# Decoder trunk on one core: sums of weights in place, more load buffers, two units without accumulating transfers, operands at one residue

## The chip, the cores and the metric

The kernel runs on one core of a Trainium2 chip. The metric is the device time of one execution in microseconds (us). The core has a matrix engine (TensorE, "PE" in the profile, its weight loads "PEld"), VectorE (DVE), ScalarE (ACT), GpSimd (POOL) and SyncE (SP), which here only issues transfers. Each engine works through its own instructions in order.

## The reference

A trunk of two layers over 512 positions of width 1024, in float32. Layer A: a recurrent mixer (norm, projection, causal convolution of width 4, gated linear recurrence, output projection) and a SwiGLU block. Then keys and values shared by what follows; layer B: dilated sliding-window attention in three groups of heads and a second SwiGLU block. The change lies in the two SwiGLU blocks and in where tiles lie in the on-chip memory.

```python
def swiglu(h, w_in, w_out):
    g, u = jnp.split(h @ w_in, 2, axis=-1)
    return (jax.nn.silu(g) * u) @ w_out
# h: 512 x 1024, w_in: 1024 x 5632, w_out: 2816 x 1024
h = h + swiglu(rms_norm(h, norm), w_in, w_out)
```

## The kernel before

**Precision.** Every matrix is split into a high and a low half (`...h`, `...l`, type fp32r), and a product is three matmuls (`mm3`, L195 to L197): high by high, high by low, low by high. For weights, ScalarE casts the high half (L114, L145, L157) and the low half is the weight minus it: on VectorE (L116, L158), on POOL, or, in the SwiGLU input weights, by a negated copy on ScalarE (L135) to which a transfer from memory adds the weight itself (L136, issued by POOL, "accumulating transfer").

**SwiGLU input products.** The 2816 hidden columns are 22 units of 128. A unit takes two blocks of weights, `g` (tile `wr`) and `u` (tile `ur`), seen as a 2 x 2 matrix A11, A12, A21, A22 in pairs of 128 rows. Seven products instead of eight give it (Winograd's scheme): A11, A12, A22 and four sums of weights S1 to S4 on the left, B11, B21, B22 and sums T1 to T4 of activations on the right; each is 4 x 3 matmuls of 256 columns. Activations lie in `xh`/`xl` (B11, T1, B21, B22) and `th`/`tl` (T2 to T4), formed by `sums` at the end of the stage before. A unit is done in three parts: `head` (A11, S1), then the `tail` (A22, S4 and the gate) of the unit before, then `middle` (S2, A12, S3). Partial results are copied out of PSUM on ScalarE (`t`, L535). The gate needs the norm's factor in a row per position, `rb`, from `norm_factors` and `norm_rows`: small VectorE work, `dg`, and a matmul by `ones`. It is formed after the `middle` of unit 0.

**SwiGLU output products.** The hidden columns come in chunks of 4, 5, 5, 4, 4 units. The out blocks of a chunk (8 blocks, 12 or 15 matmuls of 512 columns each, left operand `wh`/`wl`, right `gh`/`gl`) are spread between the units of the next chunk, mostly two after each unit; the last chunk's come at the end.

**Weights' stream.** `Stream` holds the list of pieces in the order of use. At `get(i)` it issues the load of piece i+2 (SP's queue) and the split of piece i+1. Raw weights lie in `wr` (two buffers, for units' `g`, out blocks and all other projections alike) and `ur` (one buffer); split weights in `wh`/`wl` (three each), `a2h`/`a2l` (two) and `sh`/`sl` (three). The sums are formed in two tiles `s`, (S1, S2) and (S3, S4). A framework lays out the order of every engine's instructions and the semaphores before the run, from its own estimates; a tile's buffer is free when all who read it are done.

**Where tiles lie.** Pools are stacked: `keep` (h, `xh`, `xl`, `par`, `ident`, `ones`, `ssum`), then the weights, then the stage's pool; on the other side of the memory, "right", the pools of `hgh` and of `gh`, closed by a `pad` tile of 8 floats. `Pool` rounds a tile to 64 bytes a partition.

Other stages that the profile shows: the projections of the recurrent layer (`xh` by `wh`, 512 columns), its output (`hgh`), keys, values and queries (L820 to L822: weights on the right, `xh`, or its copy by phase `xp`, on the left), attention.

Of the kernel before, what the change touches and what calls it, by code (L numbers as in the profile page):

```python
# [20 lines left out]
F32 = mybir.dt.float32  # L21
F32R = mybir.dt.float32r
# [3 lines left out]
ALU = mybir.AluOpType  # L26
# [3 lines left out]
T = 512  # L30
KB = 8
HID = 2816
HB = HID // 128
# [48 lines left out]
class Stream:  # L82
# [6 lines left out]
        self.nl = self.ns = self.halved = 0  # L89

    def _load(self, i):
        ap, kind = self.pieces[i]
        if kind == "unit":
            return self._load_unit(i)
        r = self.pool.tile([128, 1024], F32, name=f"wr{i}", tag="wr", bufs=2)
# [23 lines left out]

    def _load_unit(self, i):  # L120
        g = self.pool.tile([128, 1024], F32, name=f"wr{i}", tag="wr", bufs=2)
        u = self.unit_pool.tile([128, 1024], F32, name=f"ur{i}", tag="ur", bufs=1)
        self.raw[i] = (g, u)
        return [lambda t=t, a=a: self.nc.sync.dma_start(t, a) for t, a in zip((g, u), self.pieces[i][0])]

    def _split_unit(self, i):

        nc, pool, up = self.nc, self.pool, self.unit_pool
        g, u = self.raw.pop(i)

        def halves(t):
            return t.rearrange("q (k e c) -> q e k c", e=2, c=128)

        def negated_plus(lo, raw, ap):
            nc.scalar.mul(lo, raw, -1.0)  # L135
            nc.gpsimd.dma_start(lo, ap, accum_op=ALU.add)  # L136

        with self.tc.high_priority():
            a1h = pool.tile([128, 1024], F32R, name=f"wh{i}", tag="wh")
            a1l = pool.tile([128, 1024], F32R, name=f"wl{i}", tag="wl")  # L140
            a2h, a2l = (up.tile([128, 4, 128], F32R, name=n, tag=n, bufs=2) for n in ("a2h", "a2l"))
            (a11, a12), (a21, a22) = ([halves(t)[:, e] for e in range(2)] for t in (g, u))
            negated_plus(a1l, g, self.pieces[i][0][0])
            negated_plus(a2l, a22, halves(self.pieces[i][0][1])[:, 1])
            nc.scalar.copy(a1h, g)  # L145
            nc.scalar.copy(a2h, a22)
            s = [up.tile([128, 2, 4, 128], F32, name="s", tag="s", bufs=2) for _ in range(2)]
            sh, sl = ([up.tile([128, 2, 4, 128], F32R, name=n, tag=n, bufs=3) for _ in range(2)] for n in ("sh", "sl"))
            V = nc.vector
            for n in range(2):  # L150
                if n == 0:
                    V.tensor_tensor(s[0][:, 0], a21, a22, ALU.add)
# [4 lines left out]
                nc.scalar.copy(sh[n], s[n])  # L157
                V.tensor_tensor(sl[n], s[n], sh[n].bitcast(F32), ALU.subtract)  # L158
        a1h, a1l = halves(a1h), halves(a1l)
        self.parts[i] = {"A11": (a1h[:, 0], a1l[:, 0]), "A12": (a1h[:, 1], a1l[:, 1]), "A22": (a2h, a2l)}  # L160
        for n in range(4):
            self.parts[i][f"S{n + 1}"] = tuple(x[n // 2][:, n % 2] for x in (sh, sl))

    def start(self, n):

# [23 lines left out]
def trunk(tc, A, out):  # L189
# [8 lines left out]

    pieces = []

    def add_pieces(aps, kind=""):
        start = len(pieces)
        pieces.extend((a, kind) for a in aps)
        return start

    lru_order = [8, 9, 10, 11, 12, 0, 13, 1, 14, 2, 15, 3, 4, 5, 6, 7]
# [4 lines left out]
    def ffn_pieces(wi, wo):  # L211

        def out_step(c, m):
            c0 = 128 * sum(CHUNKS[:c])
            return "out", c, m, add_pieces([A[wo][m][:, c0:c0 + 128 * CHUNKS[c]]])
# [12 lines left out]
        return steps  # L228
# [7 lines left out]
    with tc.tile_pool(name="keep", bufs=1) as kp, tc.tile_pool(name="wts", bufs=3) as wp, \  # L236
# [94 lines left out]


        close_hg, hg = right_pool(tc, "hg")
        with tc.tile_pool(name="lru", bufs=2, reuse_waits="tile") as lp:
            lp = Pool(lp)
            for k in range(KB):
                split(h[k], gain(C_AN, k), xh[k], xl[k])
                run(split_a if k == 0 else split_b if k == 3 else ())
# [16 lines left out]
            r = norm_factors(lp)  # L355
            rb = norm_rows(lp, r, "q", 2)


            lam = par[:, C_LAM:C_LAM + 8]
            sp8, nsp8 = (lp.tile([128, 8], F32, name=n, bufs=1) for n in ("sp8", "nsp8"))  # L360
            l1 = lp.tile([128, 8], F32, name="l1", bufs=1)
            l2 = lp.tile([128, 8], F32, name="l2", bufs=1)
            l3 = lp.tile([128, 8], F32, name="l3", bufs=1)
# [133 lines left out]
        def sums(pool, m, c):  # L497

            if m % 2 == 0:
                return  # L500
            x = [pool.tile([128, T], F32, name="x", tag=t) for t in ("gt", "ut")]
            for i in range(2):
                S.activation(x[i], h[m - 1 + i], AF.Copy, scale=gain(c, m - 1 + i))
# [20 lines left out]
        def swiglu(fp, gp, steps, after):  # L524
# [21 lines left out]
            def middle(w, pa, pc, t1):  # L546

                pb = bank("S")
                product(pa, w["S2"], "T2", False, False)
                t2 = copied(pa, "t2")  # L550
                product(pb, w["A12"], "B21", True, True)
                g = fp.tile([128, T], F32, name="gt")
                u = fp.tile([128, T], F32, name="ut")
                V.tensor_tensor(g[:, a], pb[:, a], t1, ALU.add)
                product(pa, w["S3"], "T3", False, False)
                t3 = copied(pa, "t3")
                V.tensor_tensor(u[:, b], pc[:, a], t3, ALU.add)
                return w, pa, pc, t2, g, u
# [27 lines left out]
            for kind, *step in steps:  # L586
                if kind == "unit":
                    j, p = step
                    w = ws.get(p)
                    st = head(w)  # L590
                    if pending:
                        tail(*pending.pop())
                    pending.append(middle(w, *st))
                    if j == 0:
                        r = norm_factors(fp)
                        rbs.append(norm_rows(fp, r, "o"))
                    continue
                c, m, p = step
                n, last = CHUNKS[c], c == len(CHUNKS) - 1
# [529 lines left out]
```

## Time and profile before

| | |
|---|---|
| median of three runs | 1316.86 us (1315.63 to 1318.35) |
| profiled execution | 1319.34 us, span 1317.4 us |
| instructions | 19514 |
| PE / DVE / ACT / POOL busy | 92% / 72% / 53% / 20% |
| mean granted clock of TensorE | 0.965 |
| transferred | 147.89 MB, mean 112 GB/s |

A row of a group reads: line, engine, operation, tile written <- tiles read, shapes, count, then total busy time in us and mean ns of one, then the engine's idle time before them and what ended it. A row of the timeline reads: start in us, duration in us, engine, line, operation, tiles, and in brackets the idle time before it and who ended it; "SPq" is the issue of a transfer by SP. A row of stretches reads: stretch, its length, busy us and count of PE, PEld, DVE, ACT, POOL, then TensorE's clock, the share of the transfer engines, GB/s. A matmul's duration is longer than the distance to the next one, as matmuls overlap.

The first SwiGLU block runs from about 200 to 565 us, the second from about 943 to the end.

### The profile page before, as it was taken

How to read it: one execution, taken by the hardware profiler on the slowest of the kernel's cores; microseconds unless marked ns; L12 is line 12 of the kernel's file. 1: busy time of each engine (PE TensorE's matmuls, PEld its weight loads, DVE VectorE, ACT ScalarE, POOL GpSimd, SP SyncE). 2: the span in 40 equal slices, each digit the busy share in tenths (PEclk: the TensorE clock that was granted, in tenths of full speed). 3: DMA queues.
4: the chain of work that ended last, by engine and by line, in shares of the span. 5: the costliest groups of instructions: out<-in, count | busy, mean ns of one | idle time of the engine just before them, and what ended most of it. 6: DMA issues, size and time to landing. Idle time of an engine off the chain costs nothing.

```text
span 1317.4 us, 19514 instructions
## 1 busy us (share of the span) xinstructions
PE 1218.1 (92%) x7218; PEld 1066.1 (81%) x7218; DVE 954.6 (72%) x1870; ACT 701.7 (53%) x1322; POOL 269.1 (20%) x233
## 2 busy tenths in 40 slices
PE   6779897999999999998998899899889999999998
PEld 5557686988999988876777677789788889889987
DVE  7888887766777666688755666776886776677666
ACT  5466676554454555357444555655864555555531
POOL 1444001111111111020233355531211111111100
PEclk8888899999999999998998999799999999999999
DMA  5221257566766665242332212101665667666643
GB/s 177 80 64 49 80 118 165 125 145 140 159 152 152 143 143 121 74 133 68 111 97 65 76 53 65 33 17 49 128 145 120 155 149 166 143 137 145 142 101 105
DMA packets 69694, 147.89 MB, mean 112 GB/s; under 512 B 6240, under 2 KB 30944, under 8 KB 69600
## 3 DMA queue, kind: packets, MB, share of 16 engines
q1 hardware_dynamic: 39024, 110.17, 27.3%
q0 software_dynamic: 29568, 34.61, 17.9%
q10 hardware_dynamic: 1008, 1.88, 0.5%
q8 instruction: 56, 0.92, 0.3%
q14 instruction: 38, 0.31, 0.1%
HBM read 143.49 MB, written 2.10 MB: 111 GB/s over the span
## 4 chain that ended last, share of the span: by engine, by line
issue 44%; PE 25%; DVE 16%; POOL 6%; ACT 5%; DMA 3%; POOLq 0%; SPq 0%; ACTq 0%; DVEq 0%
PE ps L196 5%; PE ps L197 5%; PE ps L195 5%; POOL a2l L136 4%; DVE kn L779 3%; PE ps L820 3%; PE ps L821 3%; PE ps L822 3%; POOL wl L136 2%; DMA wl<-in_f_in 1%; DVE xc L409 1%; ACT junk L762 1%; DVE gated L458 1%; DVE wl L116 1%; ACT wh L114 1%
## 5 line engine op out<-in xcount | busy, mean ns | idle before, releaser
L114 ACT CAST wh<-wr 128x1024 fp32r<-128x1024 f32 (+2 forms) x150 | 124.4, 831 | 191.7 <-PE ps L196 82.2
L197 PE MATMUL ps<-xh,wl 128*128 128x256 f32 (+1 forms) x544 | 179.8, 330 | 14.7 <-DMA wl<-in_f_in 14.7
L195 PE MATMUL ps<-xh,wh 128*128 128x256 f32 (+1 forms) x544 | 180.2, 332 | 8.1 <-ACT xh L279 5.9
L196 PE MATMUL ps<-xl,wh 128*128 128x256 f32 (+1 forms) x544 | 178.2, 328 | 1.5 <-DVE xl L284 1.3
L116 POOL TENSOR_TENSOR wl<-wr,wh 128x1024 fp32r<-128x1024 f32 x46 | 114.2, 2484 | 241.5 <-ACT wh L114 215.3
L136 POOL DMA_DIRECT2D a2l<-in_f_in x44 | 53.0, 1205 | 434.7 <-ACT a2l L135 386.9
L196 PE MATMUL ps<-gl,wh 128*128 128x512 f32 x352 | 139.2, 396 | 0.0
L195 PE MATMUL ps<-gh,wh 128*128 128x512 f32 x352 | 138.9, 395 | 0.0
L197 PE MATMUL ps<-gh,wl 128*128 128x512 f32 x352 | 138.9, 394 | 0.0
L197 PEld LDWEIGHTS ps<-xh,wl 128*128 128x128 f32 x544 | 105.6, 194 | 26.1 <-DMA wl<-in_f_in 17.4
L195 PEld LDWEIGHTS ps<-xh,wh 128*128 128x128 f32 x544 | 105.6, 195 | 19.2 <-ACT xh L279 5.9
L196 PEld LDWEIGHTS ps<-xl,wh 128*128 128x128 f32 x544 | 105.7, 194 | 12.4 <-DVE xl L284 2.1
L158 DVE TENSOR_TENSOR sl<-s,sh 128x1024 fp32r<-128x1024 f32 x88 | 106.9, 1217 | 1.8 <-ACT sh L157 1.7
L195 PE MATMUL ps<-th,sh 128*128 128x256 f32 x352 | 103.0, 293 | 3.3 <-ACT t L535 3.1
L157 ACT CAST sh<-s 128x1024 fp32r<-128x1024 f32 x88 | 91.8, 1045 | 18.8 <-PE ps L196 12.6
L195 PE MATMUL ps<-xh,sh 128*128 128x256 f32 x352 | 99.6, 283 | 1.1 <-ACT sh L157 1.1
L197 PE MATMUL ps<-th,sl 128*128 128x256 f32 x352 | 99.9, 284 | 0.0
L196 PE MATMUL ps<-tl,sh 128*128 128x256 f32 x352 | 99.7, 283 | 0.0
L196 PE MATMUL ps<-xl,sh 128*128 128x256 f32 x352 | 99.0, 281 | 0.0
L197 PE MATMUL ps<-xh,sl 128*128 128x256 f32 x352 | 98.8, 281 | 0.0
L116 DVE TENSOR_TENSOR wl<-wr,wh 128x512 fp32r<-128x512 f32 (+2 forms) x104 | 86.0, 830 | 14.7 <-ACT wh L114 14.5
L581 DVE TENSOR_TENSOR o<-ps,rb 128x512 f32<-128x512 f32 x80 | 55.1, 689 | 54.5 <-PE ps L197 53.1
(259 smaller groups left out, 3317.3 us busy)
## 6 DMA issues: line engine op xcount, KB each, us to landing
ur<-in_f_in SPq DMA_DIRECT2D x44, 512.0 KB, 3.8
wr<-in_f_in SPq DMA_DIRECT2D x44, 512.0 KB, 4.1
wl<-in_f_in POOLq DMA_DIRECT2D x44, 512.0 KB, 6.7
wr<-in_f_out SPq DMA_DIRECT2D x48, 256.0 KB, 2.7
wr<-in_w_q SPq DMA_DIRECT2D x24, 512.0 KB, 3.6
a2l<-in_f_in POOLq DMA_DIRECT2D x44, 256.0 KB, 5.2
wr<-in_f_out SPq DMA_DIRECT2D x32, 320.0 KB, 3.4
wr<-in_w_in SPq DMA_DIRECT2D x14, 512.0 KB, 3.6
```

Source lines behind the costliest of these rows:

```text
L114: nc.scalar.copy(hi[:, c], r[:, c])
L116: eng.tensor_tensor(lo[:, c], r[:, c], hi[:, c].bitcast(F32), ALU.subtract)
L136: nc.gpsimd.dma_start(lo, ap, accum_op=ALU.add)
L157: nc.scalar.copy(sh[n], s[n])
L158: V.tensor_tensor(sl[n], s[n], sh[n].bitcast(F32), ALU.subtract)
L195: PE.matmul(ps, wh, xh, start=first, stop=False, **k)
L196: PE.matmul(ps, wh, xl, start=False, stop=False, **k)
L197: PE.matmul(ps, wl, xh, start=False, stop=last, **k)
L581: V.tensor_tensor(o, ps, rbs[0], ALU.mult)
L779: V.scalar_tensor_tensor(dst[:, c], dst[:, c], r[:, nh * t + i:nh * t + i + 1], grow[:, g_row, :], ALU.mult, ALU.mult)
L820: PE.matmul(ps[t], xh[k][:, r], wh[:, c], start=k == 0, stop=False)
L821: PE.matmul(ps[t], xh[k][:, r], wl[:, c], start=False, stop=False)
```

## The change

1. The sums S1 to S4 are formed in place in the raw tiles: a22 = a21 + a22 (S1), a21 = a11 - a21 (S3), then, once `u` has been split, a11 = a22 - a11 (S2), a12 = a12 - a11 (S4). The tiles `s` go. One pair of `sh`/`sl` holds S3 and S1, the other S2 and S4.
2. `ur` gets two buffers; out blocks get raw tiles of their own (`or`, two), so `wr` serves units and other projections alone. For room, `ut` gets one buffer, and both tiles `x` of `sums` use the two of `gt`.
3. For units 0 and 1 of each block (`early`) the low halves of A11, A12 and A22 are subtracted on VectorE, without negated copy and accumulating transfer.
4. `norm_factors` (at unit 0) and `norm_rows` (moved to unit 1, between its `head` and the `tail` of unit 0) get high priority.
5. Sizes: `par` 128 floats instead of 104, the pad on the right 88 instead of 8, `xp` 640 instead of 516; small tiles of the recurrent stage move to a pool `few` of their own. Nothing else in these stages changes.

```diff
-        tc.nc.gpsimd.memset(pool.tile([128, 8], F32, name="pad"), 0.0)
+        tc.nc.gpsimd.memset(pool.tile([128, 88], F32, name="pad"), 0.0)
...
+        if kind == "out":
+            r = self.unit_pool.tile([128, 640], F32, name=f"or{i}", tag="or", bufs=2)
+        else:
+            r = self.pool.tile([128, 1024], F32, name=f"wr{i}", tag="wr", bufs=2)
...
-        u = self.unit_pool.tile([128, 1024], F32, name=f"ur{i}", tag="ur", bufs=1)
+        u = self.unit_pool.tile([128, 1024], F32, name=f"ur{i}", tag="ur", bufs=2)
...
-        def negated_plus(lo, raw, ap):
-            nc.scalar.mul(lo, raw, -1.0)
-            nc.gpsimd.dma_start(lo, ap, accum_op=ALU.add)
+        def split(hi, lo, raw, ap):
+            nc.scalar.copy(hi, raw)
+            if ap is None or early:
+                V.tensor_tensor(lo, raw, hi.bitcast(F32), ALU.subtract)
+            else:
+                nc.scalar.mul(lo, raw, -1.0)
+                nc.gpsimd.dma_start(lo, ap, accum_op=ALU.add)
...
-            negated_plus(a1l, g, self.pieces[i][0][0])
-            negated_plus(a2l, a22, halves(self.pieces[i][0][1])[:, 1])
-            nc.scalar.copy(a1h, g)
-            nc.scalar.copy(a2h, a22)
-            s = [up.tile([128, 2, 4, 128], F32, name="s", tag="s", bufs=2) for _ in range(2)]
...
-                if n == 0:
-                    V.tensor_tensor(s[0][:, 0], a21, a22, ALU.add)
-                    V.tensor_tensor(s[0][:, 1], s[0][:, 0], a11, ALU.subtract)
-                else:
-                    V.tensor_tensor(s[1][:, 0], a11, a21, ALU.subtract)
-                    V.tensor_tensor(s[1][:, 1], a12, s[0][:, 1], ALU.subtract)
-                nc.scalar.copy(sh[n], s[n])
-                V.tensor_tensor(sl[n], s[n], sh[n].bitcast(F32), ALU.subtract)
+            split(a1h, a1l, g, aps[0])
+            split(a2h, a2l, a22, halves(aps[1])[:, 1])
+            V.tensor_tensor(a22, a21, a22, ALU.add)
+            V.tensor_tensor(a21, a11, a21, ALU.subtract)
+            split(sh[0], sl[0], u, None)
+            V.tensor_tensor(a11, a22, a11, ALU.subtract)
+            V.tensor_tensor(a12, a12, a11, ALU.subtract)
+            split(sh[1], sl[1], g, None)
...
-                steps.append(("unit", j, add_pieces([(A[wi][j], A[wi][HB + j])], "unit")))
+                steps.append(("unit", j, add_pieces([(A[wi][j], A[wi][HB + j])], "unit", j < 2)))
...
-        par = kp.tile([128, N_PAR], F32, name="par")
+        par = kp.tile([128, 128], F32, name="par")[:, :N_PAR]
...
-                xp = lp.tile([128, T + 4], F32, name="xp")
+                xp = lp.tile([128, 640], F32, name="xp")[:, :T + 4]
...
-            x = [pool.tile([128, T], F32, name="x", tag=t) for t in ("gt", "ut")]
+            x = [pool.tile([128, T], F32, name="x", tag="gt") for _ in range(2)]
...
-            tt = pool.tile([128, 3, 256], F32, name="tt", tag="s")
+            tt = pool.tile([128, 3, 256], F32, name="tt", tag="or")
...
-                u = fp.tile([128, T], F32, name="ut")
+                u = fp.tile([128, T], F32, name="ut", bufs=1)
...
                     st = head(w)
+                    if j == 1:
+                        with tc.high_priority():
+                            rbs.append(norm_rows(fp, r, "o"))
                     if pending:
                         tail(*pending.pop())
                     pending.append(middle(w, *st))
                     if j == 0:
-                        r = norm_factors(fp)
-                        rbs.append(norm_rows(fp, r, "o"))
+                        with tc.high_priority():
+                            r = norm_factors(fp)
```

More of the change, by code (lines that the diff above doesn't have):

```diff
@@ L91, in _load @@
     def _load(self, i):
-        ap, kind = self.pieces[i]
+        ap, kind = self.pieces[i][:2]
         if kind == "unit":
             return self._load_unit(i)
-        r = self.pool.tile([128, 1024], F32, name=f"wr{i}", tag="wr", bufs=2)
+        if kind == "out":
+            r = self.unit_pool.tile([128, 640], F32, name=f"or{i}", tag="or", bufs=2)
+        else:
+            r = self.pool.tile([128, 1024], F32, name=f"wr{i}", tag="wr", bufs=2)
         w = ap.shape[-1]
@@ L126, in _split_unit @@
     def _split_unit(self, i):
-        nc, pool, up = self.nc, self.pool, self.unit_pool
+        nc, V, pool, up = self.nc, self.nc.vector, self.pool, self.unit_pool
         g, u = self.raw.pop(i)
+        early = self.pieces[i][2]
         def halves(t):
             return t.rearrange("q (k e c) -> q e k c", e=2, c=128)
-        def negated_plus(lo, raw, ap):
-            nc.scalar.mul(lo, raw, -1.0)
-            nc.gpsimd.dma_start(lo, ap, accum_op=ALU.add)
+        def split(hi, lo, raw, ap):
[5 more added lines that the diff above has]
+                nc.gpsimd.dma_start(lo, ap, accum_op=ALU.add)
         with self.tc.high_priority():
@@ L141, in _split_unit, with both @@
             a2h, a2l = (up.tile([128, 4, 128], F32R, name=n, tag=n, bufs=2) for n in ("a2h", "a2l"))
+            sh, sl = ([up.tile([128, 1024], F32R, name=n, tag=n, bufs=3) for _ in range(2)] for n in ("sh", "sl"))
             (a11, a12), (a21, a22) = ([halves(t)[:, e] for e in range(2)] for t in (g, u))
-            negated_plus(a1l, g, self.pieces[i][0][0])
-            negated_plus(a2l, a22, halves(self.pieces[i][0][1])[:, 1])
-            nc.scalar.copy(a1h, g)
-            nc.scalar.copy(a2h, a22)
-            s = [up.tile([128, 2, 4, 128], F32, name="s", tag="s", bufs=2) for _ in range(2)]
-            sh, sl = ([up.tile([128, 2, 4, 128], F32R, name=n, tag=n, bufs=3) for _ in range(2)] for n in ("sh", "sl"))
-            V = nc.vector
-            for n in range(2):
-                if n == 0:
-                    V.tensor_tensor(s[0][:, 0], a21, a22, ALU.add)
-                    V.tensor_tensor(s[0][:, 1], s[0][:, 0], a11, ALU.subtract)
-                else:
-                    V.tensor_tensor(s[1][:, 0], a11, a21, ALU.subtract)
-                    V.tensor_tensor(s[1][:, 1], a12, s[0][:, 1], ALU.subtract)
[L157 to L162, printed above, removed]
+            aps = self.pieces[i][0]
+            split(a1h, a1l, g, aps[0])
[6 more added lines that the diff above has]
+            split(sh[1], sl[1], g, None)
+        def both(name, hi, lo, e):
+            self.parts[i][name] = (halves(hi)[:, e], halves(lo)[:, e])
+        self.parts[i] = {"A22": (a2h, a2l)}
+        both("A11", a1h, a1l, 0)
+        both("A12", a1h, a1l, 1)
+        both("S1", sh[0], sl[0], 1)
+        both("S3", sh[0], sl[0], 0)
+        both("S2", sh[1], sl[1], 0)
+        both("S4", sh[1], sl[1], 1)
     def start(self, n):
@@ L199, in trunk, with add_pieces @@
     pieces = []
-    def add_pieces(aps, kind=""):
+    def add_pieces(aps, kind="", early=False):
         start = len(pieces)
-        pieces.extend((a, kind) for a in aps)
+        pieces.extend((a, kind, early) for a in aps)
         return start
@@ L214, in out_step @@
             c0 = 128 * sum(CHUNKS[:c])
-            return "out", c, m, add_pieces([A[wo][m][:, c0:c0 + 128 * CHUNKS[c]]])
+            return "out", c, m, add_pieces([A[wo][m][:, c0:c0 + 128 * CHUNKS[c]]], "out")
         steps, j0 = [], 0
@@ L333, in trunk @@
         close_hg, hg = right_pool(tc, "hg")
-        with tc.tile_pool(name="lru", bufs=2, reuse_waits="tile") as lp:
+        with tc.tile_pool(name="lru", bufs=2, reuse_waits="tile") as lp, \
+                tc.tile_pool(name="few", bufs=2, reuse_waits="tile") as ls:
             lp = Pool(lp)
+            small = Pool(ls)
             for k in range(KB):
@@ L354, in trunk @@
                 squares(k, lp, "q", 2)
-            r = norm_factors(lp)
+            r = norm_factors(small)
             rb = norm_rows(lp, r, "q", 2)
             lam = par[:, C_LAM:C_LAM + 8]
[L360 to L363, printed above, removed]
+            sp8, nsp8 = (small.tile([128, 8], F32, name=n, bufs=1) for n in ("sp8", "nsp8"))
+            l1 = small.tile([128, 8], F32, name="l1", bufs=1)
+            l2 = small.tile([128, 8], F32, name="l2", bufs=1)
+            l3 = small.tile([128, 8], F32, name="l3", bufs=1)
             V.scalar_tensor_tensor(l1, lam, -1.0, lam, ALU.mult, ALU.max)
```

## The prediction

> **What bounds the kernel now.** I read the page's first part, then the waits of TensorE (PE), then busy time by stretches, then the timeline where PE stood still.
>
> ```profile
> PE 1218.1 (92%) x7218; PEld 1066.1 (81%) x7218; DVE 954.6 (72%) x1870; ACT 701.7 (53%) x1322; POOL 269.1 (20%) x233
> ...
> wl<-in_f_in POOLq DMA_DIRECT2D x44, 512.0 KB, 6.7
> ```
>
> PE is busy 92% of the span; the second line is the accumulating transfer that makes the low half of a unit's weights: 6.7 us from issue to landing. The waits of PE (us in total, times, longest) that concern the edit, over the whole span:
>
> ```profile
> PE ps L197 <- DMA wl<-in_f_in: 14.7, 13, 2.6
> ...
> PE ps L195 <- ACT t L535: 9.7, 8, 5.0
> ...
> PE ps L313 <- DVE dg L312: 2.4, 1, 2.4
> ```
>
> They sum to 26.8 us, 2% of the span. Two long stretches inside the two SwiGLU blocks, with TensorE's clock and the DMA share as the last columns but one, and the transfer wait within the first and from 1000 us on:
>
> ```profile
> 240.00:520.00 280.00, 273.35 (x1891) 251.79 (x1890) 197.39 (x320) 146.36 (x227) 36.23 (x35) 0.99 0.64 143
> 1003.00:1280.00 277.00, 269.71 (x1855) 247.47 (x1854) 192.05 (x310) 140.69 (x217) 34.70 (x34) 1.00 0.64 143
> ...
> PE ps L197 <- DMA wl<-in_f_in: 6.4, 6, 2.6
> ...
> PE ps L197 <- DMA wl<-in_f_in: 5.7, 6, 1.9
> ```
>
> Inside the blocks PE is 97% busy: only two things count there, how far apart matmuls start, and the transfer wait. The other losses are at the blocks' starts.
>
> **The starts: double buffers and no accumulating transfers for units 0 and 1.** Unit 2 of the first block, in order of time (start, duration):
>
> ```profile
> 208.10 0.33 SPq L124 DMA_DIRECT2D ur<-in_f_in  x1
> ...
> 214.13 0.69 DVE L152 TENSOR_TENSOR s<-ur 128x512 f32<-128x512 f32 x1 [2.46 <-DMA ur<-in_f_in]
> ...
> 215.95 0.47 DVE L312 TENSOR_SCALAR dg<-ident,nry 128x128 f32<-128x128 f32 x1
> ...
> 216.85 0.33 SPq L124 DMA_DIRECT2D wr<-in_f_in  x1
> ...
> 225.33 1.06 ACT L135 ACTIVATE wl<-wr 128x1024 fp32r<-128x1024 f32 x1 [5.23 <-DMA wr<-in_f_in]
> ...
> 227.22 0.36 ACT L535 COPY t<-ps 128x256 f32<-128x256 f32 x1
> ```
>
> One `ur` buffer: unit 2's load is issued at 208.10 and its first sum waits for it until 214.13. Behind that sum in VectorE's order lies `dg`, and PE waits 2.4 us for that. Then unit 4's `wr` is issued at 216.85, ScalarE waits for it until 225.33, and the copy `t`, which PE needs, stands behind it: the 5.0 us wait. With two `ur`, unit 2's load goes a unit earlier, its split ends, by my estimate, near 211 instead of 216, and unit 4's `wr` follows. In place, though, `wr` is held until its last sum is split (one cast and one subtraction more, some 2.3 us by the rows below), so I take 3.5 of the 5.0 and all of the 2.4. The norm's small work, now urgent, helps the 2.4.
>
> ```profile
> 200.00:210.00 10.00, 8.33 (x66) 7.71 (x66) 9.36 (x28) 7.15 (x12) 2.05 (x2) 1.00 0.75 134
> ...
> 220.00:230.00 10.00, 5.00 (x34) 4.79 (x33) 4.56 (x9) 4.27 (x6) 0.85 (x1) 0.76 0.79 165
> 230.00:240.00 10.00, 10.00 (x77) 9.91 (x77) 6.70 (x11) 5.46 (x10) 1.19 (x1) 0.90 0.51 107
> ...
> 940.00:950.00 10.00, 7.43 (x39) 6.69 (x38) 9.79 (x20) 10.00 (x18) 1.70 (x2) 0.83 0.76 156
> 950.00:960.00 10.00, 8.12 (x47) 7.12 (x47) 10.00 (x20) 6.37 (x13) 0.00 (x0) 0.83 0.28 52
> ```
>
> The clock reads 0.76 and 0.90 after that wait: 0.24 x 10/0.5 = 4.8 us and 2.0 us at half speed. PE resumes at 227.6, so 2.4 + 2.0 us of work ran at half, 2.2 us lost, and it goes with the wait. The other side: two units at each start now subtract on VectorE.
>
> ```profile
> L158 DVE TENSOR_TENSOR sl<-s,sh 128x1024 fp32r<-128x1024 f32 x88 | 106.9, 1217 | 1.8 <-ACT sh L157 1.7
> ...
> L152 DVE TENSOR_TENSOR s<-ur 128x512 f32<-128x512 f32 x44 | 30.4, 690 | 37.2 <-DMA ur<-in_f_in 37.2
> ...
> L145 ACT CAST wh<-wr 128x1024 fp32r<-128x1024 f32 x44 | 45.8, 1040 | 30.6 <-DMA wr<-in_f_in 26.8 <-PE ps L197 2.9 <-PE ps L196 0.9
> ...
> L135 ACT ACTIVATE wl<-wr 128x1024 fp32r<-128x1024 f32 x44 | 46.6, 1059 | 8.1 <-DMA wr<-in_f_in 8.0
> ```
>
> Per unit 1.22 + 0.69 us, 3.8 us per start, against four negated copies fewer on ScalarE and four issues fewer on POOL per start; POOL is 20% busy, and ScalarE's share of the gain I count at nothing. At the first start VectorE is 9.36 of 10 us busy, at the second 9.79 and 10.00. First start: half shows, 1.9: -2.4 - 3.5 - 2.2 + 1.9 = **-6.2** (ends: -9.6, and +3.8 if no wait goes). Second start: of the transfer wait 14.7 - 6.4 - 5.7 = 2.6 us lies there and goes; of the 9.7 us of waits for `t`, 4.7 are left beside the 5.0, and I give this start half, 2.2; all 3.8 show, as VectorE is full: -2.6 - 2.2 + 3.8 = **-1**. Ends: -4.8, and +8, because `x` now has one pair of buffers for four pairs of blocks, and three times the two copies below (1.32 us) may stand after the last read of the pair before instead of beside it.
>
> ```profile
> 945.74 1.32 ACT L503 ACTIVATE x<-h,par 128x512 f32<-128x512 f32 x2
> ```
>
> **Sums in place, out blocks with buffers of their own, one `ut`.** The sums' count stays (four, two casts, two subtractions per unit). Inside the blocks raw weights already land well ahead: what is late is the chain from the end of the product that frees `wl` (third buffer) through cast 1.04, negated copy 1.06 and the transfer's 6.7, and nothing touches it for units 2 to 21. So the 6.4 + 5.7 us stay: **0**, ends +-4 for another collision of loads. New waits: VectorE's `a22` sum waits for ScalarE's two reads of it, the `a11` sum for cast and negated copy of `wr`, hence for a free `wl`. Behind them on VectorE lie the tail's gate products and the out blocks' additions, which free PSUM for PE. From a free `wl` to the last subtraction 1.04 + 1.06 + 2 x 0.69 + 1.04 + 1.22 = 5.7 us; PE gets to S2 after S3, two out blocks, a head and a tail, 12 x 0.12 + 24 x 0.2325 + 48 x 0.12 = 12.8 us later (spacings from the rows of the next part). Covered by 7 us; without cover 5.7 us per unit. One `ut`: its next write stands behind the last read of the old one on VectorE anyway; nothing, up to 2 us at the first start.
>
> **One residue.** Every tile of the first pool is a multiple of 512 bytes but `par`, 104 floats rounded to 448 bytes. So weights, sums and `th` lie 64 bytes short of `xh` (64 against 128 mod 512), and `gh`, on the right, at 448. Afterwards all lie at 128. Spacing in runs without a gap, first and last matmul of each (96, 74, 43, 24, 12 and 24 matmuls):
>
> ```profile
> 543.18 0.40 PE L195 MATMUL ps<-gh,wh 128*128 128x512 f32 x1
> ...
> 565.25 0.40 PE L197 MATMUL ps<-gh,wl 128*128 128x512 f32 x1
> ...
> 720.13 0.40 PE L821 MATMUL ps<-wl,xh 128*128 128x512 f32 x1
> ...
> 737.16 0.39 PE L822 MATMUL ps<-wh,xl 128*128 128x512 f32 x1
> ...
> 600.71 0.40 PE L822 MATMUL ps<-wh,xp 128*128 128x512 f32 x1
> ...
> 610.27 0.40 PE L822 MATMUL ps<-wh,xp 128*128 128x512 f32 x1
> ...
> 406.54 0.28 PE L195 MATMUL ps<-xh,wh 128*128 128x256 f32 x1
> ...
> 409.25 0.28 PE L197 MATMUL ps<-xh,sl 128*128 128x256 f32 x1
> ...
> 527.59 0.28 PE L195 MATMUL ps<-th,a2h 128*128 128x256 f32 x1
> ...
> 528.91 0.28 PE L197 MATMUL ps<-th,a2l 128*128 128x256 f32 x1
> ...
> 976.53 0.28 PE L195 MATMUL ps<-xh,sh 128*128 128x256 f32 x1
> ...
> 979.14 0.28 PE L197 MATMUL ps<-xh,wl 128*128 128x256 f32 x1
> ```
>
> 512 columns: 22.07/95 = 232.3 ns (`gh`), 17.03/73 = 233.3 (`w` on `xh`), and 9.56/42 = 227.6 where both operands are at 64 already (`w` on `xp`). 256 columns: 117.8 at unequal residues, 120 at equal ones, and once, after a stop, 113.5 with the same tiles that else run at 117.8. So one residue looks good for 512 columns and bad for 256. Counts:
>
> ```profile
> L195 PE MATMUL ps<-gh,wh 128*128 128x512 f32 x352 | 138.9, 395 | 0.0
> ...
> L820 PE MATMUL ps<-wh,xh 128*128 128x512 f32 x224 | 93.5, 418 | 0.8 <-DVE o L581 0.8
> ```
>
> `gh`: 3 x 352 x 4.7 ns = -5.0; `w` on `xh`: 3 x 224 x 5.7 = -3.8, half of it where PE isn't the bound, -1.9; the in and out projections I leave at nothing. 256 columns: four of seven products use `xh`: 44 x 4 x 12 = 2112 matmuls x 2 ns = +4.2 at the price of `th`, the nearest row with equal residues. Some pairs at 64 in attention run nearer 118, so I take +2. Sum **-5**. Ends: +4 (nothing at 512), and -8.8 - 2112 x 4.3 - 1584 x 6.5 = -28 us, if everything of 256 columns fell to 113.5.
>
> The Trainium skill speaks against this term: "SBUF — State Buffer", section "Who interferes with whom", says that PE never waits on another reader, and "TensorE: Matmul & The Clock Gate", section "Step-by-step: what each phase is for", that loading the next weights takes nothing from the running matmul's reads. By that, addresses could not matter and the term would be 0, which is rival B below. The rows disagree: 233.3 against 227.6 ns for the same weights and shape.
>
> **Sum.** -6.2 - 1 + 0 - 5 = -12.2 us. The profiled execution took 1319.34 us (span 1317.4), 0.19% above the median of 1316.86; taken off the median: **1305 us**.
>
> **Rivals.** (B) Spacing does not depend on the operands' residue, the differences belonging to the products themselves: only the starts' -7.2, 1310 us. For it: 113.5 and 117.8 for the same tiles. Against it: `xp` differs from `xh` in nothing but address. (C) All 256-column products fall to 113.5: -7.2 - 28 = -35, 1282 us. For it: the run at 976 us; against: `th`, at equal residues already, shows 120. (D) The starts' stalls only move, behind ScalarE's next raw weights, and the subtractions show, 1.9 + 3.8 us, against -5: 1317.5 us, no change. For it: VectorE full at 950 us. (E) Slower: the in-place sums, which now wait for a free `wl`, reach PE late in every unit with out blocks. It decides once queueing on VectorE and ScalarE eats the 7 us; 0.5 us beyond that in 36 units is +18, 1323 us. For it: VectorE runs 70% busy there; against: 7 us is much.
>
> **How the numbers follow.** Forecast 0.42, B 0.15, C 0.15, D 0.15, E 0.13. The forecast's own range is 1296 to 1313. 0.2% (2.6 us) is about what a measurement here tells from no change. Faster: forecast, B, C and a quarter of D, 0.76; same: the rest of D, 0.11; slower: E, 0.13. Range 1281 to 1319: C's value at the low end, D's above it, E left out.
>
> **What would show it.** In the profile after: VectorE 8 instructions more, ScalarE 8 fewer, POOL transfers 80; no wait for `dg`, the ScalarE wait before 230 us under 2 us and the clock at 1 there (first term); the wait for `wl` still near 12 us (the zero); `gh` runs at 227 to 228 ns and `xh` runs of 256 columns at 118 to 120 (residue). Wrong would make it: a new wait of PE on a subtraction of the sums (E), VectorE's additions at 940 to 960 us pushing PE's start back by more than 4 us (D), or 256-column runs under 115 ns (C).

## The result, and the profile after

The changed kernel takes 1355.68 us (median of four, 1352.64 to 1358.38), the kernel before on the same chip 1317.61 us (1315.63 to 1324.34): 1.028 times as long (95%: 1.0235 to 1.0324). It is 38 us slower where 12 us faster was forecast, and outside the range.

First, of the kernel after: PE's busy line and the transfer that makes the low half, from the page; then PE's waits over the whole span (us in total, times, longest).

```profile
PE 1233.0 (91%) x7218; PEld 1081.9 (80%) x7218; DVE 960.4 (71%) x1878; ACT 692.9 (51%) x1314; POOL 259.5 (19%) x225
...
wl<-in_f_in POOLq DMA_DIRECT2D x40, 512.0 KB, 7.2
```

```profile
PE ps L207 <- DMA wl<-in_f_in: 37.7, 25, 3.4
...
PE ps L205 <- ACT t L547: 2.0, 3, 1.2
...
PE ps L323 <- DVE dg L322: 0.5, 1, 0.5
```

The wait for `dg` went from 2.4 to 0.5 us, that for `t` from 9.7 to 2.0. The wait that the prediction had put at "near 12" went from 14.7 us in 13 waits to 37.7 in 25, and the transfer itself from 6.7 to 7.2 us.

The same two stretches as before, with some from the two starts (TensorE's clock is the last column but two), and the waits within the long ones:

```profile
200.00:210.00 10.00, 7.49 (x46) 6.63 (x44) 9.01 (x19) 9.15 (x17) 1.00 (x1) 0.80 0.56 129
...
210.00:220.00 10.00, 9.32 (x48) 8.21 (x47) 5.56 (x23) 3.42 (x7) 0.00 (x0) 0.69 0.11 28
...
220.00:230.00 10.00, 9.95 (x81) 9.56 (x80) 7.33 (x11) 7.14 (x10) 2.07 (x2) 1.00 0.53 97
...
240.00:520.00 280.00, 264.91 (x1791) 243.69 (x1790) 187.13 (x305) 136.82 (x214) 34.14 (x33) 0.98 0.62 140
...
960.00:970.00 10.00, 4.91 (x20) 3.81 (x18) 9.33 (x18) 6.95 (x11) 0.87 (x1) 0.69 0.63 146
970.00:980.00 10.00, 9.16 (x37) 7.43 (x38) 8.80 (x33) 5.45 (x10) 0.00 (x0) 0.63 0.09 26
...
1003.00:1280.00 277.00, 257.07 (x1727) 236.61 (x1726) 184.62 (x298) 134.15 (x210) 34.19 (x33) 0.98 0.61 141
```

```profile
PE ps L207 <- DMA wl<-in_f_in: 15.1, 10, 3.0
...
PE ps L207 <- DMA wl<-in_f_in: 19.1, 12, 3.4
```

In the same 280 us PE now does 1791 matmuls instead of 1891. The waits in these stretches are 34.2 us against 12.1. Seven of the eight waits of 2.2 us or more are followed by a stretch of 3.41 us at half clock (one such stretch before), 1.7 us lost each.

**Where the 39 us of span went.** For each block I took the time from its first product to its last matmul, less 118 ns for each matmul of 256 columns and 227 for each of 512 (the cheap spacings): what is left is loss. "Start" is the part until 252 matmuls of 256 columns (three units) are done, "steady" the rest. The same reckoning for the kernels that follow (us; from the one trace of each):

| kernel | start 1 | steady 1 | start 2 | steady 2 |
|---|---|---|---|---|
| before | 13.4 | 16.2 | 13.9 | 16.6 |
| after | 12.9 | 32.3 | 18.6 | 35.3 |
| before, casts first | 9.9 | 30.8 | 14.8 | 28.3 |
| after, order tied | 12.9 | 8.0 | 17.4 | 8.3 |
| the same, no early subtractions | 8.5 | 7.8 | 16.3 | 8.0 |
| the same, operands shifted | 6.6 | 4.7 | 14.2 | 5.1 |

After against before: -0.5 + 16.1 + 4.7 + 18.7 = +39.0; the few small matmuls of the norm, left out of the reckoning, give 1.6, the stages ahead of the first block +0.4, those between -1.8. So nearly all of it lies in the steady parts, which the prediction had at 0 and -5.

**One unit, before and after.** Before, then after, in order of time (start, duration, engine, line, tiles; SPq and POOL DMA rows are issues of transfers):

```profile
432.59 0.28 PE L197 MATMUL ps<-xh,wl 128*128 128x256 f32 x1
...
432.96 1.06 ACT L135 ACTIVATE wl<-wr 128x1024 fp32r<-128x1024 f32 x1
...
433.92 1.04 ACT L145 CAST wh<-wr 128x1024 fp32r<-128x1024 f32 x1
...
434.32 0.86 POOL L136 DMA_DIRECT2D wl<-in_f_in  x1 [3.17 <-ACT wl L135]
...
434.99 0.33 SPq L98 DMA_DIRECT2D wr<-in_f_out  x1
```

```profile
441.33 0.28 PE L207 MATMUL ps<-xh,wl 128*128 128x256 f32 x1
...
441.60 1.04 ACT L140 CAST wh<-wr 128x1024 fp32r<-128x1024 f32 x1
...
442.54 1.06 ACT L144 ACTIVATE wl<-wr 128x1024 fp32r<-128x1024 f32 x1
...
443.63 0.69 DVE L159 TENSOR_TENSOR wr<-ur,wr 128x512 f32<-128x512 f32 x1 [0.21 <-ACT wl L144]
...
443.89 0.86 POOL L145 DMA_DIRECT2D wl<-in_f_in  x1 [4.03 <-ACT wl L144]
...
444.35 0.33 SPq L127 DMA_DIRECT2D ur<-in_f_in  x1
...
449.85 0.28 PE L205 MATMUL ps<-xh,wh 128*128 128x256 f32 x1
...
451.10 0.39 PE L207 MATMUL ps<-xh,wl 128*128 128x256 f32 x1 [0.85 <-DMA wl<-in_f_in]
```

Two things differ. Before, the negated copy comes first and the cast behind it; after, the cast is first, and the negated copy starts 0.93 us behind the end of the product that frees `wl` (its last read starts at 441.33) instead of 0.10 (last read at 432.59). And the in-place sum L159, the last reader of `ur`, waits for the negated copy, ends 0.4 us behind the transfer's issue and so frees `ur`: a load of 512 KB starts 0.46 us behind the accumulating transfer. (Before, it was an out block's load of 256 or 320 KB, 0.67 us behind.) This transfer takes 7.2 us, those of the units around it 7.2 to 7.4; before, in the units from 433 to 484 us, 6.0 to 6.7.

The sum of it: from the last read's end to the landing 0.93 + 1.06 + 0.29 + 7.3 = 9.6 us; PE is back at `wl` after S3 and two out blocks, 8.5 us with blocks of five units and 7.2 with four. That leaves waits of 1.1 and 2.4 us; the trace has 0.9 to 1.1, and 2.1 to 3.4. Before, 0.10 + 1.06 + 0.29 + 6.3 to 6.7 = 7.8 to 8.2 us: just covered with five, not with four.

### The profile page after: what moved, and what is told of

Read it like the earlier page. It is cut to its first block, busy times and chain, and to the rows that moved or that the text cites. A ratio compares the mean times of both kernels' runs of the same rounds, so it can differ in the third digit from the quotient of the medians.

```text
span 1356.6 us, 19447 instructions
## 1 busy us (share of the span) xinstructions
PE 1233.0 (91%) x7218; PEld 1081.9 (80%) x7218; DVE 960.4 (71%) x1878; ACT 692.9 (51%) x1314; POOL 259.5 (19%) x225
## 5 line engine op out<-in xcount | busy, mean ns | idle before, releaser
L207 PE MATMUL ps<-xh,wl 128*128 128x256 f32 (+1 forms) x544 | 183.7, 338 | 38.2 <-DMA wl<-in_f_in 37.7
L206 PE MATMUL ps<-xl,wh 128*128 128x256 f32 (+1 forms) x544 | 182.2, 335 | 1.9 <-DVE xl L294 1.7
L156 DVE TENSOR_TENSOR ur<-ur 128x512 f32<-128x512 f32 x44 | 32.6, 741 | 153.6 <-ACT a2l L144 153.5
L145 POOL DMA_DIRECT2D a2l<-in_f_in x40 | 48.1, 1202 | 414.3 <-ACT a2l L144 414.3
L206 PEld LDWEIGHTS ps<-xl,wh 128*128 128x128 f32 x544 | 108.3, 199 | 13.9 <-DVE xl L294 4.1
L206 PE MATMUL ps<-xl,sh 128*128 128x256 f32 x352 | 104.2, 296 | 3.9 <-DVE xl L294 3.9
L205 PE MATMUL ps<-xh,sh 128*128 128x256 f32 x352 | 103.9, 297 | 2.9 <-DVE h L339 1.5
L207 PE MATMUL ps<-xh,sl 128*128 128x256 f32 x352 | 103.8, 295 | 0.8 <-DVE sl L142 0.8
L117 ACT CAST wh<-wr 128x1024 fp32r<-128x1024 f32 (+1 forms) x70 | 71.4, 1021 | 64.2 <-PE ps L837 17.7
L835 PE MATMUL ps<-wh,xh 128*128 128x512 f32 x224 | 92.1, 412 | 0.8 <-DVE o L593 0.8
L547 ACT COPY t<-ps 128x256 f32<-128x256 f32 x132 | 48.2, 366 | 85.0 <-PE ps L207 77.9
L837 PE MATMUL ps<-wh,xl 128*128 128x512 f32 x224 | 88.6, 396 | 0.2 <-DVE xl L290 0.2
```

The source lines that it names most:

```text
L117: nc.scalar.copy(hi[:, c], r[:, c])
L156: V.tensor_tensor(a22, a21, a22, ALU.add)
L205: PE.matmul(ps, wh, xh, start=first, stop=False, **k)
L206: PE.matmul(ps, wh, xl, start=False, stop=False, **k)
L207: PE.matmul(ps, wl, xh, start=False, stop=last, **k)
L547: S.copy(t, ps[:, a])
```

## The experiments

Theory A: the order of cast and negated copy is the loss. Theory B: the loads that the in-place sums release beside the transfer are. Ratios are to the kernel before, with 95% intervals; "wait" is PE's for `wl`.

**1. The lines swapped back (swap_order).** In `split` of the kernel after:

```diff
-            nc.scalar.copy(hi, raw)
-            if ap is None or early: ...
-            else: negated copy, accumulating transfer
+            if not (ap is None or early): negated copy, accumulating transfer
+            nc.scalar.copy(hi, raw)
+            if ap is None or early: ...
```

> The kernel after with one thing turned back: in each unit's split the negated copy and its accumulating transfer are issued ahead of the cast of the high half, as in the kernel before. Theory A (the order is the loss): in the kernel after the cast (1.04 us) stands ahead of the negated copy, which starts 0.92 us after the product that frees wl where before it was 0.10 us; turned back it starts at 0.10 us, PE's wait for the transfer falls from 37.7 us to under 10, the half-clock stretches that follow the waits go too, and the time is 1305 to 1317 us. Theory B (collision: the in-place sum frees ur 0.5 us behind the transfer's issue, so a 512 KB load of ur runs beside the transfer, which takes 7.2 instead of 6.3 to 6.7 us): the transfer stays at 7.2 us or more, the time stays above 1345 us. Both by about half: 1322 to 1335 us.

1353.27 us, 1.029 (1.0258 to 1.0321), wait 35.9 us. This tells nothing of A or B: the framework, which lays out each engine's order itself, still put the cast first in 34 of 40 units. In the kernel before, the written order had stood in 33 of 44. `wh` comes free one matmul ahead of `wl`, which lets the cast go first; why the framework's estimates do so here and not there is not shown.

**2. The casts first in the kernel before (before_cast_first).**

```diff
-            negated_plus(a1l, g, ...); negated_plus(a2l, a22, ...)
-            nc.scalar.copy(a1h, g); nc.scalar.copy(a2h, a22)
+            nc.scalar.copy(a1h, g); negated_plus(a1l, g, ...)
+            nc.scalar.copy(a2h, a22); negated_plus(a2l, a22, ...)
```

> The kernel before with the casts of A11/A12 and of A22 issued ahead of their negated copies, nothing else. Theory A (order is the whole loss): every unit with out blocks gets a wait, 1355 us or more (none of the change's gains is in it). Theory B (collision alone): transfers stay at 6.3 to 6.7 us, the shift of 0.94 us is mostly within the slack of 0 to 0.7 us, 1317 to 1325 us. Both: 13 waits get 0.94 us each and some 10 units with 0.65 us of slack get 0.3 each, 15 us, and 5 to 8 us at half clock: 1332 to 1341 us.

1342.21 us, 1.0208 (1.0178 to 1.0237): 26 us for the order of two instructions, with none of the change's other parts. Wait and transfer of this kernel:

```profile
PE ps L197 <- DMA wl<-in_f_in: 37.5, 25, 3.3
```

```profile
wl<-in_f_in POOLq DMA_DIRECT2D x44, 512.0 KB, 6.7
```

The wait is that of the kernel after. "Both" was right in kind and a little low in size. The two causes are not cleanly apart here: between 433 and 497 us the out block's load is now issued 0.27 us ahead of the transfer instead of 0.67 us behind it, and the transfer takes 6.5 to 7.5 us instead of 6.0 to 6.7, so the order moves the collision too.

**3. The order tied (tied_order).** As 1, and the cast is made to depend on the negated copy, so that the layout can't put it first (`add_manual_dep(cast, negated copy)`).

> The kernel after with the negated copy tied ahead of the cast in all 40 units (swapping the two lines alone had left the cast ahead in 34 of 40). Theory A (order): the negated copy starts 0.10 us behind the product that frees wl instead of 0.92; 25 waits lose 0.8 to 0.9 us each, PE's wait for the transfer falls from 37.7 to about 15 us, some 10 us at half clock go as well: 1318 to 1333 us. Theory B (the load of ur beside the transfer): the transfer, moved up, still meets the load, takes 7.5 us or more, waits stay above 30 us and the time above 1345.

1304.84 us, 0.9909 (0.9884 to 0.9934): 51 us less than after, and faster than before. Its timeline, the transfer, and the two long stretches:

```profile
442.49 0.28 PE L209 MATMUL ps<-xh,wl 128*128 128x256 f32 x1
...
442.86 1.05 ACT L144 ACTIVATE wl<-wr 128x1024 fp32r<-128x1024 f32 x1
...
443.80 1.03 ACT L146 CAST wh<-wr 128x1024 fp32r<-128x1024 f32 x1
...
444.20 0.86 POOL L145 DMA_DIRECT2D wl<-in_f_in  x1 [3.58 <-ACT wl L144]
...
444.87 0.69 DVE L161 TENSOR_TENSOR wr<-ur,wr 128x512 f32<-128x512 f32 x1 [0.19 <-ACT wh L146]
...
445.59 0.33 SPq L127 DMA_DIRECT2D ur<-in_f_in  x1
...
451.31 0.28 PE L209 MATMUL ps<-xh,wl 128*128 128x256 f32 x1
```

```profile
wl<-in_f_in POOLq DMA_DIRECT2D x40, 512.0 KB, 5.5
```

```profile
240.00:520.00 280.00, 279.98 (x1933) 257.93 (x1932) 202.68 (x328) 145.38 (x230) 36.20 (x35) 1.00 0.65 150
...
1003.00:1280.00 277.00, 276.92 (x1891) 254.22 (x1891) 197.20 (x321) 138.42 (x220) 33.01 (x32) 1.00 0.61 140
```

PE is busy for all but 0.02 us of the first stretch and has no wait for `wl` anywhere. It did better than either theory alone allowed, because the one order sets both: the negated copy starts 0.09 us behind the release, and the last reader of `wr` is now the cast, for which the in-place sum L161 waits, so that L161 ends, and the load of `ur` starts, 1.39 us behind the transfer's issue instead of 0.46. With that head start the transfer takes 5.5 us, as if alone. Chain: 0.09 + 1.05 + 0.29 + 5.5 = 6.9 us, under both 7.2 and 8.5. The Trainium skill, "DMA: Bandwidth & Descriptors", section "Queues, rings and completion order", says that a transfer engine takes turns between the queues that have work for it, packet by packet; the trace agrees in that a load from another queue slows the transfer (7.2 against 5.5 us). Taking turns alone does not give the 5.5 us of the tied order, where the load is issued 4.1 us before the transfer lands and does not slow it; how the head start acts is not shown.

**4. Loads later, order as it is (late_loads), and both (tied_late_loads).** A unit's loads are made to follow the out block's load on SP's queue:

```diff
+            self.tc.add_manual_dep(unit_load, self.last_out, ...)
```

> The kernel after with its order of cast and negated copy, but each unit's two loads are put behind the loads of the out blocks on SP's queue, so that none starts in the first 5 us of the accumulating transfer. Theory A: nothing changes, 1350 us or more. Theory B: the transfer takes 5.4 to 5.7 us, as in the units of the kernel after where no load runs beside it, instead of 7.2; waits of 1.2 us each vanish, 1310 to 1325 us.

1325.03 us, 1.0057 (1.0032 to 1.0081); transfer and wait:

```profile
wl<-in_f_in POOLq DMA_DIRECT2D x40, 512.0 KB, 5.5
```

```profile
PE ps L226 <- DMA wl<-in_f_in: 16.3, 18, 2.1
```

So the collision is worth some 30 us by itself, close to B's value; what is left is the order's 0.8 us a unit.

> Both edits together. If order and collision are all of the loss, the wait for the transfer is under 5 us and the time 1300 to 1315 us, where the prediction had the kernel after. If a third cause takes part (the starts, the 256-column spacing, sums in place), 1320 us or more.

1313.26 us, 0.9973 (0.9959 to 0.9988), wait 2.4 us: no third cause of size, but 8 us slower than the order tied alone. Later loads cost something of their own (steady losses 12.4 and 13.4 against 8.0 and 8.3); in the trace PE has waits of 3.1 us for `t`, 2.5 for `gh` and 2.4 for `wl` in the steady parts, where the tied kernel has none. What brings them on is not shown.

**5. The order tied in the kernel before (before_tied).**

> The kernel before with the negated copy tied ahead of the cast in all 44 units (it stands so in 33 already), nothing else. Theory C (order and transfer explain the tied kernel's gain as well; the change's other parts bring little): the 11 units with the cast first lose their waits, the 14.7 us of waits fall to 7 or less, and 2 to 4 us at half clock go: 1305 to 1312 us. Theory D (the gain of the tied kernel comes from the change's own parts, buffers, early subtractions, residue): the wait stays above 11 us, 1314 us or more.

1310.95 us, 0.9943 (0.9923 to 0.9963), nearer to C by its time; but C's step is wrong:

```profile
PE ps L203 <- DMA wl<-in_f_in: 13.8, 13, 3.1
```

```profile
wl<-in_f_in POOLq DMA_DIRECT2D x44, 512.0 KB, 6.6
```

The wait did not fall. The transfer stays at 6.6 us, as an out block's load still starts beside it. So the order alone does not give the 5.5 us: it came only together with the change's buffers and in-place sums, and with the other order the same parts make 7.2. Which of these parts it needs, and where this kernel's 6 us come from, is not shown.

**6. Sums only in `ur` (tied_u_sums); a second pair of `x` (tied_u_x).** S2 is written over S1 and S4 over S3, so no sum waits for `wr`'s split; then also every second pair of `x` takes `ut` and `rb`.

```diff
-            V.tensor_tensor(a11, a22, a11, ALU.subtract)
-            V.tensor_tensor(a12, a12, a11, ALU.subtract)
-            split(sh[1], sl[1], g, None)
+            V.tensor_tensor(a22, a22, a11, ALU.subtract)
+            V.tensor_tensor(a21, a12, a22, ALU.subtract)
+            split(sh[1], sl[1], u, None)
```

> Tied order, and all four sums are formed in the ur tile (S2 over S1, S4 over S3, after S1 and S3 are split), so no sum waits for the cast and the negated copy of wr, and ur comes free without them. Theory of the prediction's rival E (sums that wait for a free wl reach PE late or hold up VectorE): faster than tied_order by 5 us or more. Theories A and B: within 5 us of tied_order, as the load of wr still follows the cast and runs beside the transfer.

1304.56 us, 0.9906 (0.9884 to 0.9928), 0.3 us from the tied kernel: sums that wait for a free `wl` cost nothing that can be measured.

> The tied kernel with all four sums in ur, and with the second and fourth pair of x tiles in ut and rb, free at that time, instead of waiting for the first pair's. Theory: in the kernel after PE stands 4 to 4.6 us at the second start for VectorE's xl, because x has one pair of buffers; with two pairs that stall falls under 2 us and the half-clock stretch behind it goes: 1296 to 1301 us. Rival (VectorE is full there, 9.8 of 10 us busy, so the stall stays): 1303 to 1305 us, like the same kernel without it.

1304.04 us, 0.9898 (0.9879 to 0.9917), second start 14.1 against the 14.8 of `tied_u_sums`: the rival holds, `x`'s buffers are not what PE waits for there. What is: VectorE and PE of the kernel after at the second start,

```profile
957.21 1.23 DVE L142 TENSOR_TENSOR sl<-wr,sh 128x1024 fp32r<-128x1024 f32 x1
958.34 1.23 DVE L142 TENSOR_TENSOR wl<-wr,wh 128x1024 fp32r<-128x1024 f32 x1
959.48 1.23 DVE L142 TENSOR_TENSOR sl<-ur,sh 128x1024 fp32r<-128x1024 f32 x1
...
963.61 0.43 DVE L294 TENSOR_TENSOR xl<-t,xh 128x256 fp32r<-128x256 f32 x1
```

```profile
964.09 0.58 PE L206 MATMUL ps<-xl,sh 128*128 128x256 f32 x1 [3.86 <-DVE xl L294]
```

The weights' subtractions, an early one among them, stand on VectorE ahead of the activations' `xl`, for which PE waits 3.9 us.

**7. No early subtractions (tied_no_early).** `early` is always False.

> The tied kernel, but units 0 and 1 of each block also go by accumulating transfers. The prediction's first two terms gave early subtractions a cost on VectorE of 1.9 and 3.8 us and a gain of 2.6 us and a part of 6.2: by that, 1303 to 1310 us. Rival: without them the first units wait for transfers of 5.5 us plus negated copy, 8 us or more in all, 1312 us or more.

1300.82 us, 0.9874 (0.9853 to 0.9895), under the 1303 to 1310 expected. It is 4 us below the tied kernel, though the intervals overlap: the early subtractions gain nothing and look like a loss. The starts' losses go from 12.9 to 8.5 and from 17.4 to 16.3, but the time at half clock differs as well, 10.2 against 3.4 us at the first start and 10.2 against 13.7 at the second.

**8. The residue (before_residue, after_old_residue, tied_no_early_old).** Only `par` and the pad get the new sizes, in the kernel before; or the old ones, in the two others.

> The kernel before with the sizes alone (par 128, pad 88): xh, weights, sums, th and gh all at 128 mod 512. Theory A: spacings 227 ns at 512 columns (before 232 to 233) and 120 at 256 columns on xh (before 118); sum -5.0 -1.9 +4.2 = -2.7 us, of which the shorter out blocks give back 0.11 to 0.14 us in each of the 13 waits for the transfer: 1315 to 1317 us, hardly to be told from no change. The prediction's term: -5, 1312.6 us. Rival: spacing does not hang on addresses, nothing changes in the spacings.

1314.82 us, 0.9996 (0.9979 to 1.0013): nothing. Medians over all matmuls: `gh` by weights 232 to 227 ns, `w` by `xh` 234 to 227, `xh` of 256 columns 118 to 120; the wait went from 14.7 to 16.4 us.

> The kernel after with par and pad of their old sizes, so weights and th 64 short of xh and gh at another residue again (xp stays at 640). Theory A: spacings back to 232 and 118, time 1355 to 1358 us, as the longer out blocks also cover 0.1 us more of each of the 25 waits. Rival (the slowdown comes from the 256-column matmuls at equal residues): 1340 us or less.

1355.59 us, 1.0315 (1.0286 to 1.0344): as the kernel after. Equal addresses are not the slowdown.

> The tied kernel without early subtractions, with the old sizes of par and pad, so gh at 232 and xh at 118 ns again. The prediction's term says 5 us slower, 1306 us; by the spacings read since (-5.0 at 512 columns, -1.9 half of it bound, +4.2 at 256 columns) 2 to 3 us slower, 1302 to 1304 us. Rival (theory that only the 256 columns count, the PE's 512-column blocks being covered): 2 to 4 us faster, 1297 to 1299 us.

1302.53 us, 0.9903 (0.9874 to 0.9933): 1.7 us above 7, and the intervals overlap.

**9. The rule of addresses (residues, skew, before_skew).** In the first, 64 bytes lie between the eight `xh` and between the eight `xl` of the kernel before.

> The kernel before with 64 bytes between the eight xh tiles and between the eight xl tiles, so that against the weights at 64 they lie at differences of 64, 128, 192, 256, 320, 384, 448 and 0. Its time says nothing new; its spacings are to show whether only equality counts: 256 columns 120 ns at difference 0 and 118 at all others, 512 columns 227 at 0 and 232 to 235 at others. Rival: the spacing hangs on the difference step by step, or on the product and not on the address (no pattern over k).

1317.29 us in its one run. Spacing at full clock by the place of the moving tile less that of the weights (medians in ns, 167 to 261 matmuls each):

| bytes mod 512 | 0 | 64 | 128 | 192 | 256 | 320 | 384 | 448 |
|---|---|---|---|---|---|---|---|---|
| 256 columns | 113 or 119 | 118 | 120 | 116 | 114 or 119 | 118 | 120 | 116 |

Not equality: the medians repeat every 256 bytes. But the difference alone does not settle it: at 0 and 256 the two values belong to different ones of the three matmuls, and in 7, where the difference is 0 throughout, the median is 120. For the next two, `th` is shifted by a small tile ahead of it, and `par` and pad are sized so that `xh`, `xl`, `th`, `tl` lie at 128 and weights, sums and `gh` at 192 (difference 192 mod 256); `skew` has this on top of 7, `before_skew` alone.

> The tied kernel without early subtractions, with the moving operands of 256 columns (xh, xl, th, tl) at 128 mod 512 and the weights and sums at 192, so that moving minus stationary is 192 mod 256, and gh at 192 too, so that 512 columns keep difference 0. Theory F (the run with spread residues: medians 113 or 119 at difference 0, 118 at 64, 120 at 128, 116 at 192, the same again 256 further): 256 columns at 116 ns instead of 120, 3.8 ns x 3696 = 14 us less than without the shift, 1284 to 1291 us. Rival (only equality counts, the pattern is another of the products): 118 ns, 1293 to 1297 us; or nothing, 1301 us.

1297.85 us, 0.9862 (0.9831 to 0.9893), the fastest of all, but its interval overlaps that of 7, and the time is just above the rival's 1293 to 1297. Two runs without a gap, 11 and 10 matmuls:

```profile
434.53 0.28 PE L208 MATMUL ps<-xl,wh 128*128 128x256 f32 x1
...
435.70 0.28 PE L209 MATMUL ps<-xh,wl 128*128 128x256 f32 x1
...
439.31 0.28 PE L209 MATMUL ps<-th,sl 128*128 128x256 f32 x1
...
440.33 0.28 PE L209 MATMUL ps<-th,sl 128*128 128x256 f32 x1
```

117 and 113 ns; over all, means of 117.0 (`xh`) and 116.3 (`th`) against 119.9 and 120.0 in 7. Theory F holds in direction; the gain, 3 us of 14, doesn't show in full. The profiled execution alone, 1291.8 us of span against 1299.7, has the losses of the table above; its other runs were slower, and why is open.

> The kernel before with the same places of the operands, nothing else. Theory F: xh 118 to 116 (2112 matmuls, 1.8 ns, 3.8 us), th 120 to 116 (1584, 3.8 ns, 6.0 us), gh 232 to 227 (1056, 5 us): -14.8, of which the shorter out blocks and products give back up to 4 us in waits for the transfer: 1302 to 1308 us. Rival (waits take all of it, as with one residue): 1314 to 1318 us.

1309.92 us, 0.996 (0.9939 to 0.9981): 5 us of the 15.

## Why the prediction was wrong

**The zero for the blocks' steady parts is the step that failed.** It says "what is late is the chain ... through cast 1.04, negated copy 1.06 and the transfer's 6.7, and nothing touches it". The chain was named in the order of the kernel after and taken for that of the kernel before, whose negated copy came first; the diff shows the two lines trade places, and the prediction passed over it. Its cover was never worked out for `wl` either, as it was for the sums: 8.5 and 7.2 us against a chain of 7.8 to 8.2 leave 0.3 to 0.7 us or nothing, so nearly all that is added to this chain is paid in every unit. Ends of +-4 "for another collision of loads" held a mechanism that, with the order, moved 16 to 19 us in each block. Shown by 2, 3 and 4.

**The sums in place.** The margin held: PE's longest wait for their subtraction (`sl`) is 0.8 us, once in the whole trace, and 6 moves nothing. Rival E had the right sign and named the in-place sums, but by another path: they reach PE in time, and harm through the load that they release.

**The first start.** Its signs came: `dg` 0.5 us, `t` 2.0, the clock 1.00 at 220 to 230 us. Yet the start's loss only went from 13.4 to 12.9, not by 6.2. What failed here is the 2.2 us at half speed of which the prediction says "it goes with the wait": the time at half clock came earlier and grew. PE now waits 4.5 us for `h`, `xh` and `xl` between 199 and 212 us (before, 1.6 us of waits lie there), and the clock reads 0.80 and 0.69 from 200 to 220 us: 10.2 us at half speed, 5.1 lost, against 6.8 and 3.4 before. How long it lasts differs between traces: `after_old_residue`, the same kernel but for sizes of tiles, has 3.4 us at half clock and 9.8 us of loss at this start. The early subtractions' 1.9 us is not the term that was far off: of the 4.4 us between 3 and 7, half clock makes 3.4, and 1.0 is left for them.

**The second start.** -1 was forecast, +4.7 came, within its ends. Of the rise, 3.4 us is half clock, for which the prediction has no term here: 0.69 and 0.63 from 960 to 980 us make 13.6 us at half speed, against 6.8 before; what sets its length is not shown. "All 3.8 show" is not far off for the early part: without it 1.1 us go, though the time at half clock rises (by 1.7 us lost), so about 2.8 by itself, an estimate from these two traces. The reason for +8, one pair of buffers for `x`, is not borne out by 6.

**One residue.** The spacings came as read, 227 and 120 ns; the sum of -5 did not. The 256 columns cost their full 4.2 us where +2 was taken, the waits grew by 1.7, and the gain at `w` on `xh` lies beside other bounds. The Trainium skill, "SBUF — State Buffer", section "Who interferes with whom", says that PE never waits on another reader, by which the term would be 0: the time of `before_residue` agrees (0.9996), its spacings do not (232 to 227 and 118 to 120 ns, by sizes of tiles alone).

That the tied kernel takes 1304.84 us, the forecast's number, is chance: its gain is 16.5 us in the steady parts, where -5 had been put, less 3.0 at the starts, where -7.2 had been.

## What to carry to other kernels

Where a chain from "buffer free" to "data needed" is as long as the work that covers it, work out its cover before anything else, and read a diff for the order of instructions on that chain: 1 us a unit came to 26 us. Ask what each buffer that comes free will load, and when: the same buffers were worth 7.2 or 5.5 us of a transfer's time by 0.9 us in the moment of release. Where a framework lays out the order, look at the order in the trace, not in the source; tie what matters.

## What the runs showed of the hardware

- In the units between 433 and 497 us an accumulating transfer of 512 KB takes 5.3 to 5.6 us where the next load is issued 1.4 us behind it (order tied, with and without early subtractions), 6.0 to 6.7 beside a load of 256 or 320 KB issued 0.67 us behind it (before), and 7.2 to 7.4 beside 512 KB issued 0.46 us behind it (after).
- Over the steady parts of all traces here, a stretch at half clock, of 3.41 us, came with 19 of the 23 waits of PE of 2.4 us or more, with 11 of the 17 from 1.75 to 2.4 us, and with none of the shorter ones; so the length of the wait alone does not decide it.
- Medians of the distance from one matmul of 256 columns to the next lie between 113 and 120 ns, and change with where the operands lie: 118 at a difference of 64 bytes mod 256, 120 at 128, 116 at 192. At 0 they are 113 or 119 in one kernel and 120 in another.
